# Decoder layer on one core: blocks of the SwiGLU product read ahead of its last writes, weight sums in place, more staging tiles, another order of rooms and of the mixer's first units, a late last norm

## The chip, the core and the metric

The kernel runs on one core of one Trainium2 chip, as one program. The metric is the device time of one execution in microseconds. Three executions of the kernel before gave 2348.09, 2351.1 and 2352.93 us; their median is 2351.1 us. A further execution was profiled, and all rows of the trace come from that one.

## The reference, cut to what matters

The layer has a batch of one, 1024 tokens and 1024 features, all float32:

```python
mod = silu(c) @ w_ada + b_ada                      # nine vectors of 1024: shifts, scales, gates
h = modulate(rmsnorm(x, norm_ffn1), sh1, sc1)
x = x + 0.5 * g1 * swiglu(h, ffn1_w_gate, ffn1_w_up, ffn1_w_down)
h = modulate(rmsnorm(x, norm_mix), sh2, sc2)
x = x + g2 * hybrid_mixer(h, ...)                  # Mamba-2 heads beside latent attention heads
h = modulate(rmsnorm(x, norm_ffn2), sh3, sc3)
x = x + 0.5 * g3 * swiglu(h, ffn2_w_gate, ffn2_w_up, ffn2_w_down)
return rmsnorm(x, norm_final)

def swiglu(h, w_gate, w_up, w_down):               # hidden width 2816
    return (silu(h @ w_gate) * (h @ w_up)) @ w_down
```

## The kernel before, in words

**Arithmetic.** Activations lie transposed: features on the 128 partitions, tokens in the columns, in two halves of 512. Each float32 operand is split in a high part (a cast on ScalarE, L173 for weights) and a low part (a subtraction, L174, on VectorE or, where the caller says so, GpSimd). `mm3` (L182 to L184) makes one product of three passes: high by high, high by low, low by high.

**Seven products for eight.** The two SwiGLU layers group features and tokens in 2x2 blocks and form seven block products. `weight_blocks` (L419 to L440) loads two weight tiles with `raw` (L155 to L160, issued by SP into a ring of four), makes four sums of weight blocks on VectorE (L426) into two tiles `comb`, and splits the blocks on demand: products 1 and 2 together, 6 with 5, 7 with 4, and 3 alone. `seven` (L442 to L489) holds the seven units of twelve matmuls; sums go to a gate result in `g` or an up result in `t`. `gate_up` (L503 to L620) runs over ten pairs of hidden tiles; the last two units of a half are held back behind the first unit of the next. `made` (L529) and `put` (L517) turn the seven sums of each result into high (`gh`, three tiles, L521) and low parts and GpSimd writes both to DRAM (`ab`, L526), 256 KB a write, 14 writes a pair. `pending` holds the puts; two leave after each unit.

**From gate/up to down.** When the last pair is through, the pool of gate/up tiles is closed, `open_down` (L145) opens the weight rooms anew, and `down` (L622) reads the seven blocks of the first of three chunks back, 2 MB each, on GpSimd's queue (`block`, L634 to L639): in the first layer blocks 1, 2, 7 and 4 go to the rooms `bh0`, `bl0`, `bh1`, `bl1` and blocks 6, 5, 3 to `d0`, `d1`, `d2` of the down pool; in the second layer block 1 goes to `d0`, 7 and 4 to `d1` and `d2`, and 2, 6, 5, 3 to `bh1`, `bh0`, `bl0`, `bl1`. The down weights (`r11`, `r21`, `r12`, `r22`, four tiles each, L646) and the residual (L653) come on SP's queue. The units of `down` run in the order of the products 1, 2, 6, 5, 3, 7, 4, four units each; each ends with a gated addition to the residual (L675). The last tokens' half of the second layer is done in two quarters of 256 columns, and each quarter splits its weights anew.

**Rooms.** All rooms are at fixed addresses. The weight pool ends at the top of the memory: before, its gate/up form is 56 KB a partition (`whi`, `wlo`, `comb`, `raw` from low to high) and its down form 44 KB (`r12`, `r22`, `r21`, `wlo`, `whi`, `r11`), so that `r11` lies where `raw` 2 and 3 were. In the second layer the tile that keeps an operand of product 6, `s2`, lies in the gate/up pool at the address that `d0` takes later.

**Side work.** Generators (`side`) are stepped once per unit. `ada_half` (L235, with `ada_add`, L227) loads four tiles of `w_ada` through the same ring `raw`, adds them up on VectorE and ends with small matmuls (L212). `to_mixer` (L1055) writes the new residual out, forms the norm's sums (squares on ScalarE L260, additions on VectorE L264), and makes the normed tiles (L327, L332, L336; for the odd tiles of the first half the low part is GpSimd's, L335, behind an extra ScalarE pass L334). `mixer` (L1118) begins with three weight tiles of 12 matmuls a half-depth for each half of the tokens. `finish` (L1080) scales the first half of the output (L1075), `finish_quarter` the two quarters of the other half.

**Order.** Except in the startup, the order of each engine's instructions is set when the program is built: a planner takes the instructions in the order of the code, with its own estimates of their times, and puts on each engine the first that it thinks is ready. `issue_after` pins a piece of code behind a given instruction of its engine.

## Time and profile before

| what | us |
|---|---|
| median of three executions | 2351.1 |
| the profiled execution | 2346.23 |
| its span, first to last instruction | 2344.5 |
| TensorE (PE) busy in it | 2143.8 |
| VectorE (DVE) busy | 1651.7 |
| ScalarE (ACT) busy | 978.2 |

All times of the trace are counted from the start of the span. The run of stages, by the trace: startup and the first gate/up to 554 us, its down part to 790, the mixer to about 1600, the second gate/up to 2054, its down part and the final norm to 2344.5. Matmuls overlap, so that the time between the starts of two of them, and not the length shown, is what one costs.

### The profile page before, as it was taken

Reading aid. Unit: us, or ns where it says so; the run is one execution under the profiler, and the core shown is the slowest. Engines: PE = TensorE matmul, PEld = TensorE weight load, DVE = VectorE, ACT = ScalarE, POOL = GpSimd, SP = SyncE. Lnnn points to the kernel's source line nnn. Section 1 sums busy time; section 2 is a strip of 40 time slices with the busy share of each in tenths; the row PEclk is TensorE's granted clock in tenths of the full one; section 3 lists DMA queues with packets and bytes.
Section 4 is the critical chain, followed back from the end, with each engine's and each line's share of the span. In section 5 each row is a group of like instructions: output and inputs, shape, how many; then the busy total and the mean of one; then the engine's idle time right before and its main releaser. Section 6 shows DMA issues by size and latency. Waiting matters only on the chain.

```text
span 2344.5 us, 27933 instructions
## 1 busy us (share of the span) xinstructions
PE 2143.8 (91%) x10095; PEld 1745.7 (74%) x10095; DVE 1651.7 (70%) x2797; ACT 978.2 (42%) x1665; POOL 312.7 (13%) x498
## 2 busy tenths in 40 slices
PE   5788999998899799999999999998999999939996
PEld 4666777776688578877778898887777777728875
DVE  7978667675566875456986888869866666545666
ACT  4523444442222442376533767525444444312223
POOL 4111112121000200000212011100111212110000
PEclk9889999999999899999999999999999999969997
DMA  8077645449953343235554000231654545497522
GB/s 292 15 232 231 198 126 171 122 149 345 356 203 120 130 149 107 77 113 173 178 195 123 17 15 22 105 129 60 195 160 130 166 126 171 154 392 260 188 101 72
DMA packets 148345, 367.31 MB, mean 157 GB/s; under 512 B 14080, under 2 KB 39040, under 8 KB 142832
## 3 DMA queue, kind: packets, MB, share of 16 engines
q1 hardware_dynamic: 89200, 182.34, 24.0%
q0 software_dynamic: 54448, 175.60, 22.3%
q10 hardware_dynamic: 4560, 7.60, 0.9%
q8 instruction: 79, 1.29, 0.2%
q14 instruction: 58, 0.48, 0.1%
HBM read 260.69 MB, written 104.79 MB: 156 GB/s over the span
## 4 chain that ended last, share of the span: by engine, by line
PE 40%; issue 35%; DVE 10%; DMA 7%; POOL 6%; ACT 1%; POOLq 0%; SPq 0%; DVEq 0%; ACTq 0%
PE mm L182 7%; PE mm L184 7%; PE mm L183 7%; PE dn L184 5%; PE dn L183 5%; PE dn L182 5%; POOL ab L526 5%; DMA d<-ab 2%; DMA raw<-w_ada 1%; DMA r<-wd 1%; PE dn L1761 1%; DVE acc L891 1%; DVE t L233 1%; DVE wlo L174 1%; DMA M<-ac_d 1%
## 5 line engine op out<-in xcount | busy, mean ns | idle before, releaser
L183 PE MATMUL mm<-bl,whi 128*128 128x512 f32 x1012 | 397.7, 393 | 4.2 <-DVE bl L389 4.2
L182 PE MATMUL mm<-bh,whi 128*128 128x512 f32 x924 | 370.8, 402 | 26.2 <-ACT g L456 11.4
L184 PE MATMUL mm<-bh,wlo 128*128 128x512 f32 x924 | 360.6, 394 | 7.6 <-DVE wlo L174 7.6
L182 PEld LDWEIGHTS mm<-bh,whi 128*128 128x128 f32 x924 | 175.2, 190 | 77.7 <-ACT g L456 15.6
L173 ACT CAST whi<-raw 128x1024 fp32r<-128x1024 f32 (+3 forms) x158 | 136.9, 882 | 225.8 <-PE mm L183 134.8
L183 PEld LDWEIGHTS mm<-bl,whi 128*128 128x128 f32 x1012 | 192.1, 190 | 43.0 <-DVE bl L389 5.1
L182 PE MATMUL dn<-bh,whi 128*128 128x512 f32 x484 | 192.6, 400 | 19.6 <-ACT whi L173 17.3
L184 PEld LDWEIGHTS mm<-bh,wlo 128*128 128x128 f32 x924 | 175.1, 190 | 46.7 <-DVE wlo L174 9.1
L173 ACT CAST whi<-r 128x512 fp32r<-128x512 f32 (+1 forms) x152 | 88.4, 583 | 255.3 <-PE dn L183 119.1
L184 PE MATMUL dn<-bh,wlo 128*128 128x512 f32 x484 | 191.6, 396 | 1.2 <-POOL wlo L174 1.2
L174 DVE TENSOR_TENSOR wlo<-raw,whi 128x1024 fp32r<-128x1024 f32 (+2 forms) x147 | 148.2, 1018 | 47.0 <-ACT whi L173 46.7
L526 POOL DMA_DIRECT2D ab<-gh x154 | 82.0, 533 | 691.3 <-ACT gh L521 677.7
L174 DVE TENSOR_TENSOR wlo<-comb,whi 128x1024 fp32r<-128x1024 f32 x80 | 97.8, 1222 | 104.6 <-ACT whi L173 104.6
L183 PE MATMUL dn<-bl,whi 128*128 128x512 f32 x396 | 157.6, 398 | 4.9 <-DVE bl L330 2.4
L173 ACT CAST whi<-comb 128x1024 fp32r<-128x1024 f32 x80 | 84.2, 1053 | 135.8 <-PE mm L183 125.4
L521 ACT CAST gh<-g 128x512 fp32r<-128x512 f32 x154 | 93.7, 621 | 112.6 <-DVE g L515 77.4
L182 PE MATMUL mm<-x,whi 128*128 128x512 f32 x280 | 115.4, 413 | 12.0 <-ACT g L456 9.8
L182 PEld LDWEIGHTS dn<-bh,whi 128*128 128x128 f32 x484 | 93.3, 193 | 40.8 <-ACT whi L173 18.5
L182 PE MATMUL dn<-d,whi 128*128 128x512 f32 (+1 forms) x200 | 76.5, 383 | 45.5 <-DMA d<-ab 45.0
L184 PE MATMUL mm<-x,wlo 128*128 128x512 f32 x280 | 110.9, 397 | 0.0
L183 PE MATMUL mm<-x,whi 128*128 128x512 f32 x280 | 110.8, 396 | 0.0
L184 PEld LDWEIGHTS dn<-bh,wlo 128*128 128x128 f32 x484 | 92.8, 192 | 21.4 <-POOL wlo L174 1.9
(379 smaller groups left out, 5009.4 us busy)
## 6 DMA issues: line engine op xcount, KB each, us to landing
ab<-gh POOLq DMA_DIRECT2D x154, 256.0 KB, 3.5
ab<-g POOLq DMA_DIRECT2D x154, 256.0 KB, 3.4
raw<-w_ada SPq DMA_DIRECT2D x56, 512.0 KB, 4.2
d<-ab POOLq DMA_DIRECT2D x12, 2048.0 KB, 13.6
raw<-wg SPq DMA_DIRECT2D x44, 512.0 KB, 5.5
raw<-wu SPq DMA_DIRECT2D x44, 512.0 KB, 4.5
r<-wd SPq DMA_DIRECT2D x64, 256.0 KB, 7.8
bl<-ab POOLq DMA_DIRECT2D x8, 2048.0 KB, 10.5
```

The source lines that it names most:

```text
L173: self.made = nc.scalar.copy(out=hi, in_=r)
L174: (engine or nc.vector).tensor_tensor(out=lo, in0=r, in1=hi.bitcast(F32), op=ALU.subtract)
L182: nc.tensor.matmul(out=out, lhsT=ah, rhs=bh, start=first and i == 0, stop=False, skip_group_check=skip)
L183: nc.tensor.matmul(out=out, lhsT=ah, rhs=bl, start=False, stop=False, skip_group_check=skip)
L184: nc.tensor.matmul(out=out, lhsT=al, rhs=bh, start=False, stop=last and i == n - 1, skip_group_check=skip)
L233: engine.scalar_tensor_tensor(out=acc, in0=r, scalar=cj, in1=acc, op0=ALU.mult, op1=ALU.add)
L521: nc.scalar.copy(out=hi, in_=x)
L526: nc.gpsimd.dma_start(out=ab[c][n - 1, :, k, i], in_=y)
L891: nc.vector.scalar_tensor_tensor(out=acc, in0=r, scalar=c, in1=acc, op0=ALU.mult, op1=ALU.add)
L1761: nc.tensor.transpose(out=pt[:, kk * 256 + b * P:kk * 256 + b * P + P], in_=Pt[b][:, (2 * k2 + kk) * P:(2 * k2 + kk + 1) * P], identity=se ...
```

## The change

- Block reads: a pool `lasting` around gate/up and down holds `s2`; it is the room of block 6 in the first layer and of block 1 in the second. Before the last pair's held units the code now reads blocks 1, 2, 6 (first layer), or 1 and 2 and, one unit later, 6 and 5 (second layer). One step of `pending` is left out there.
- Weight sums: made after the split of products 1 and 2, in place in the two raw tiles, with one half-size tile `z` for product 5. Pairs split together are now 1 and 2, 6 and 4, 7 and 3; 5 is alone.
- Rooms: `comb` is 2 KB instead of 4 KB, `gh` has five tiles instead of three, and the down rooms lie in the order `r12`, `r21`, `wlo`, `r22`, `r11`, `whi`. `r11` then lies over `raw` 0, 1 and half of 2, `whi` over the rest of `raw`.
- `ada_half` yields twice more ahead of its matmuls; the burst of steps at the first pair is 15 instead of 11.
- Mixer: the first step of the second half's norm comes behind the splits of the first two weight tiles; the six first units run tile by tile on the lower half of the depth, then on the upper; GpSimd makes no low parts of the norm any more.
- End: the second quarter reuses the split weights of the first (eight casts and eight subtractions less); the scaling of the first half is pinned behind the last subtraction of the first quarter.

The diff, cut to its core:

```diff
-SPREAD = ((1, 3, 5, 7), ())
+SPREAD = ((), ())
@@ open_weights, open_down
-                self.wts.tile([P, size], dt, name=name, bufs=bufs)
+                self.wts.tile([P, 512 if name == "comb" else size], dt, name=name, bufs=bufs)
-        for name, dt, bufs in (("r12", F32, 4), ("r22", F32, 4), ("r21", F32, 4), ("wlo", F32R, 3), ("whi", F32R, 3), ("r11", F32, 4)):
+        for name, dt, bufs in (("r12", F32, 4), ("r21", F32, 4), ("wlo", F32R, 3), ("r22", F32, 4), ("r11", F32, 4), ("whi", F32R, 3)):
@@ ada_half
             yield
+        yield
+        yield
         self.ada_finish(m, half * 4, 4, acc)
@@ weight_blocks
-        ta, tb = [self.wts.tile([P, 1024], F32, name="comb", bufs=2).rearrange("p (a b) -> p a b", b=P) for _ in range(2)]
+        z = self.wts.tile([P, 512], F32, name="comb", bufs=2).rearrange("p (a b) -> p a b", b=P)
-        tt(tb[:, 0:4], b22, b12, ALU.subtract)
-        tt(ta[:, 0:4], tb[:, 0:4], b11, ALU.add)
-        tt(ta[:, 4:8], b12, b11, ALU.subtract)
-        tt(tb[:, 4:8], b21, ta[:, 0:4], ALU.subtract)
-                src, names = next(x for x in ((r1, (1, 2)), (ta, (6, 5)), (tb, (7, 4)), (b22, (3,))) if n in x[1])
+                src, names = next(x for x in ((r1, (1, 2)), (r1, (6, 4)), (z, (5,)), (r2, (7, 3))) if n in x[1])
+                if n == 1:
+                    tt(z, b12, b11, ALU.subtract)
+                    tt(b12, b22, b12, ALU.subtract)
+                    tt(b11, b12, b11, ALU.add)
+                    tt(b21, b21, b11, ALU.subtract)
@@ ffn (block moved here from down), gate_up
+        with self.tc.tile_pool(name=f"lasting{b}", bufs=1, reuse_waits="tile") as bp:
+            def block(c, n, dp=None):
+                if n is None:
+                    return bp.tile([P, KT, 512], F32R, name="s2")
+                name = homes[n]
+                t = (bp if name == "s2" else dp if name[0] == "d" else self.main).tile([P, KT, 512], F32R, name=name)
+                v = t.rearrange("p (k h) n -> p k h n", h=2)
+                self.nc.gpsimd.dma_start(out=v[:, 0:CHUNKS[c]], in_=ab[c][n - 1])
-                hi = tp.tile([P, 512], F32R, name="gh", bufs=3)
+                hi = tp.tile([P, 512], F32R, name="gh", bufs=5)
-                        for _ in range(11):
+                        for _ in range(15):
-        self.weave(held, [side, out])
+        for f in early:
+            f()
+        self.weave(held[:1], [side])
+        for f in early2:
+            f()
+        self.weave(held[1:], [side, out])
@@ down: unit, end
+                elif (n, p) in kept:
+                    hi, lo = kept[n, p]
+                elif w < 512:
+                    np_ = CHUNKS[c]
+                    if p == 0:
+                        kept[n] = self.main.tile([P, KT, 512], F32R, name="bl0") if n == 7 else block(None, None)
+                    t = kept[n].rearrange("p (q i) n -> p q i n", i=2)[:, p, :, 0:np_ * P].rearrange("p i (a b) -> p i a b", b=P)
+                    hi, lo = kept[n, p] = t[:, 0], t[:, 1]
+                    nc.scalar.copy(out=hi, in_=r(src[n]))
+                    self.last_lo = tt(lo, r(src[n]), hi.bitcast(F32), ALU.subtract)
+            self.all_split = self.last_lo.ins
             u = rest(256, 256)
@@ run
-        homes = {1: (0, "bh0"), 2: (0, "bl0"), 6: (1, "d0"), 5: (1, "d1"), 3: (1, "d2"), 7: (0, "bh1"), 4: (0, "bl1")}
+        homes = {1: "bh0", 2: "bl0", 6: "s2", 5: "d1", 3: "d2", 7: "bh1", 4: "bl1"}      # early: ((1, 2, 6), ())
-        next(last)
-        homes = {1: (1, "d0"), 2: (0, "bh1"), 6: (0, "bh0"), 5: (0, "bl0"), 3: (0, "bl1"), 7: (1, "d1"), 4: (1, "d2")}
+        homes = {1: "s2", 2: "bh1", 6: "bh0", 5: "bl0", 3: "bl1", 7: "d1", 4: "d2"}      # early: ((1, 2), (6, 5))
@@ finish, mixer
-        yield from self.write(xT, c0, w, r[0])
+        while self.all_split is None:
+            yield
+        yield from self.write(xT, c0, w, r[0], after=self.all_split)
+            next(norm_h1)
-                self.weave(unit(0) + unit(1) + unit(2), [self.paced(norm_h1, NORM1)] if hh == 0 else [], drain=True)
+                self.weave([u for us in zip(unit(0), unit(1), unit(2)) for u in us], [self.paced(norm_h1, NORM1)] if hh == 0 else [], drain=True)
```

## Rows read from the trace of the kernel before

**Rows 1.** The page: busy us of each engine, its share of the span, instructions.
```profile
PE 2143.8 (91%) x10095; PEld 1745.7 (74%) x10095; DVE 1651.7 (70%) x2797; ACT 978.2 (42%) x1665; POOL 312.7 (13%) x498
```
**Rows 2.** PE's waits, whole run: total us, times, longest us.
```profile
PE dn L182 <- DMA d<-ab: 45.0, 2, 38.0
PE mm L182 <- ACT g L456: 21.2, 20, 2.1
PE dn L182 <- ACT whi L173: 17.7, 3, 14.1
...
PE dn L184 <- DVE wlo L174: 11.6, 7, 6.0
...
PE dn L212 <- DVE t L233: 9.0, 6, 2.9
```
**Rows 3.** Windows: length, busy PE, PEld, DVE, ACT, POOL; PE clock, DMA share, GB/s.
```profile
300.00:500.00 200.00, 194.62 (x841) 155.72 (x840) 132.70 (x185) 85.60 (x126) 36.98 (x70) 1.00 0.48 145
...
554.00:606.00 52.00, 38.07 (x137) 28.98 (x136) 37.43 (x95) 13.46 (x24) 11.16 (x21) 0.87 1.08 408
2054.00:2097.00 43.00, 5.03 (x14) 3.71 (x13) 14.80 (x23) 5.93 (x10) 8.97 (x17) 0.56 1.09 410
790.00:810.00 20.00, 4.74 (x12) 3.06 (x11) 17.72 (x17) 12.60 (x19) 10.31 (x7) 0.57 0.53 201
2309.00:2344.00 35.00, 15.24 (x87) 14.20 (x86) 20.67 (x59) 6.48 (x16) 4.77 (x6) 0.63 0.34 120
```
**Rows 4.** Timeline of PE, 2030 to 2110: start, length, instruction, idle before.
```profile
2039.34 0.39 PE L184 MATMUL mm<-s,wlo 128*128 128x512 f32 x1
...
2092.37 0.77 PE L182 MATMUL dn<-d,whi 128*128 128x512 f32 x1 [37.97 <-DMA d<-ab]
2092.94 0.63 PE L183 MATMUL dn<-d,whi 128*128 128x512 f32 x1
2093.36 0.63 PE L184 MATMUL dn<-d,wlo 128*128 128x512 f32 x1
...
2099.41 0.39 PE L183 MATMUL dn<-d,whi 128*128 128x512 f32 x1
2099.64 0.39 PE L184 MATMUL dn<-d,wlo 128*128 128x512 f32 x1
```
**Rows 5.** Timeline of POOL, 2070 to 2080: the read of block 1.
```profile
2074.04 0.54 POOL L638 DMA_DIRECT2D d<-ab  x1
```
**Rows 6.** Timeline of SP, 2036 to 2075: residual, then down weights.
```profile
2037.04 10.87 SPq L653 DMA_DIRECT2D x<-x_d  x16
2048.29 25.79 SPq L646 DMA_DIRECT2D r<-wd  x16
```
**Rows 7.** DMA issues, 2030 to 2110: count, KB each, median us to landing.
```profile
d<-ab POOLq DMA_DIRECT2D x4, 2048.0 KB, 19.4
```
**Rows 8.** The loads of the down weights (L646), 2036 to 2100.
```profile
DMA to landing us min/median/max: 7.3/9.6/19.6
```
**Rows 9.** Timeline of ACT, 796 to 806: first casts of the mixer's weights.
```profile
803.29 2.92 ACT L173 CAST whi<-raw 128x1024 fp32r<-128x1024 f32 x3
```
**Rows 10.** Groups by line, 785 to 805: busy us, mean ns, idle before.
```profile
L327 DVE SCALAR_TENSOR_TENSOR t<-x,scl,rs 128x512 f32<-128x512 f32 x8 | 7.8, 1004 | 0.1
...
L336 DVE SCALAR_TENSOR_TENSOR bl<-t,mod,bh 128x512 fp32r<-128x512 f32 x4 | 3.0, 740 | 0.0
```
**Rows 11.** Groups by line, 2309 to 2316: the first half's scaling.
```profile
L1075 DVE SCALAR_TENSOR_TENSOR x<-x,kv,rs 128x512 f32<-128x512 f32 x8 | 5.4, 747 | 0.4 <-ACT rs L303 0.4
L174 DVE TENSOR_TENSOR wlo<-r,whi 128x384 fp32r<-128x384 f32 x3 | 1.6, 549 | 0.0
```
**Rows 12.** Groups by line and shape, 400 to 440 (one pair): weights.
```profile
L174 DVE TENSOR_TENSOR wlo<-comb,whi 128x1024 fp32r<-128x1024 f32 x4 | 4.9, 1223 | 6.4 <-ACT whi L173 6.4
...
L173 ACT CAST whi<-comb 128x1024 fp32r<-128x1024 f32 x4 | 4.2, 1054 | 7.8 <-PE mm L183 7.8
...
L426 DVE TENSOR_TENSOR comb<-raw 128x512 f32<-128x512 f32 x4 | 2.7, 687 | 2.4 <-DMA raw<-wg 2.3
```

More of the change, by code (lines that the diff above doesn't have):

```diff
@@ L66 @@
 WPOOL = (12, 13)
-SPREAD = ((1, 3, 5, 7), ())
+SPREAD = ((), ())
 CHUNKS = (4, 4, 3)
+NG = 8
 TWO_PI = 2.0 * math.pi
@@ L529, in made @@
         def made(a, k, p):
-            new = lambda: tp.tile([P, 512], F32, name="g", bufs=8)
+            new = lambda: tp.tile([P, 512], F32, name="g", bufs=NG)
             if k == (0, 1):
@@ L554, in act @@
         def act(ps, t, hh):
-            a = first[t, hh] = tp.tile([P, 512], F32, name="g", bufs=8)
+            a = first[t, hh] = tp.tile([P, 512], F32, name="g", bufs=NG)
             nc.scalar.activation(out=a, in_=ps[0], func=AF.Silu)
@@ L570, in gateup @@
             return [g, u]
-        A = begin(load, gateup_mm, act, gateup, tp)
+        A = begin(load, gateup_mm, act, gateup, bp, tp)
         sums = self.made.ins
         def gate_units(t):
-            us, res = self.seven(A, self.weight_blocks(wg, t), lambda: tp.tile([P, 512], F32, name="g", bufs=8))
+            us, res = self.seven(A, self.weight_blocks(wg, t), lambda: tp.tile([P, 512], F32, name="g", bufs=NG))
             def silu(k):
@@ L620, in gate_up, with down @@
         self.weave([], [side], drain=True)
-    def down(self, ab, xd, wd, b, dp, side, mid, quarters, homes):
+    def down(self, A, block, xd, wd, b, side, mid, quarters):
         nc = self.nc
@@ L632, in down @@
         src = {1: "r11", 2: "r21", 5: "r11", 3: "r22", 7: "r12", 4: "r21"}
-        def block(c, n):
-            pool, name = homes[n]
-            t = (dp if pool else self.main).tile([P, KT, 512], F32R, name=name)
-            v = t.rearrange("p (k h) n -> p k h n", h=2)
-            nc.gpsimd.dma_start(out=v[:, 0:CHUNKS[c]], in_=ab[c][n - 1])
-            A[n] = [(v[:, k, 0], v[:, k, 1]) for k in range(CHUNKS[c])]
         def weights(c, name):
@@ L676, in unit @@
             return go
-        for f in ((block, 1), (weights, "r11"), (block, 2), (weights, "r21"), (block, 6), (weights, "r12"), (weights, "r22")):
-            f[0](0, f[1])
+        for n in (1, 2, 6):
+            if n not in A:
+                block(0, n)
+            for name in {1: ("r11",), 2: ("r21",), 6: ("r12", "r22")}[n]:
+                weights(0, name)
         for n in (1, 6):
             residual(n)
-        block(0, 5)
-        residual(5)
-        block(0, 3)
-        residual(4)
-        block(0, 7)
-        block(0, 4)
+        for n in (5, 3, 7, 4):
+            if n not in A:
+                block(0, n)
+            if n in (5, 4):
+                residual(n)
         then = {5: "r11", 3: "r22", 7: "r12", 4: "r21"}
@@ L1019, in rest, with go @@
             return [(t[:, 4 * i:4 * i + 4, 0:512], t[:, 4 * i:4 * i + 4, 512:1024]) for i in range(2)]
-        def go(load, gateup_mm, act, gateup, tp):
-            s2 = tp.tile([P, KT, 512], F32R, name="s2", bufs=1)
+        def go(load, gateup_mm, act, gateup, bp, tp):
+            s2 = bp.tile([P, KT, 512], F32R, name="s2")
             blocks = self.second_half(xT, r1[0], 0, hT, (s2[:, 0:4], s2[:, 4:8]), rest, tp)
@@ L1040, in rest, with go @@
             return [(x[:, 0:4], x[:, 4:8]) for x in t]
-        def go(load, gateup_mm, act, gateup, tp):
+        def go(load, gateup_mm, act, gateup, bp, tp):
             load(0)
             load(1)
-            s2 = tp.tile([P, KT, 512], F32R, name="s2", bufs=1)
+            s2 = bp.tile([P, KT, 512], F32R, name="s2")
             for hh in range(2):
@@ L1059, in to_mixer, with write @@
         yield from self.ada_norm(xT, 1, hh, self.hT, tp, spread=SPREAD[hh])
-    def write(self, xT, c0, w, r, scaled=(), behind=None):
+    def write(self, xT, c0, w, r, scaled=(), behind=None, after=None):
         nc = self.nc
@@ L1067, in write @@
                 yield
-            after = self.tailed.get(behind)
+            after = self.tailed.get(behind, after)
             with self.tc.issue_after(after) if after is not None and j not in scaled else nullcontext():
```

33 lines of the change are left out of this document (19 added, 14 removed).

## The prediction

> **What bounds the kernel now.** I read the page first: PE is busy for 91% of the span, no other engine for more than 70% [rows 1]. So only time in which PE stands still, or runs at the lower clock, can be won, and I looked next at who PE waits for [rows 2]. Five entries matter: 45.0 us for blocks read back, nearly all in one wait of 38.0; 17.7 for weight casts, 14.1 of it in one wait; 11.6 for low parts, 6.0 in one; 9.0 for the sums of `ada_half`; and 21.2 in twenty waits of about 1 us, one in each pair of the gate/up loops. The windows then show these places against the steady loop [rows 3]. To read them I need the price of a matmul: at the full clock the starts are 0.23 us apart, right after the long wait 0.42 [rows 4]. That is the granted clock's lower level, 1.2 GHz instead of 2.4, after PE had stood still. In the steady loop 841 matmuls x 0.23 are 193 of 200 us: little to win. The handover from gate/up to down of the first layer has 137 x 0.23 = 31.5 us of work in 52, so 20.5 are lost; that of the second 14 x 0.23 = 3.2 in 43, so 39.8 are lost; the mixer's entry 2.8 in 20, so 17.2. In both handovers the DMA engines are full, at 408 and 410 GB/s.
>
> **Second handover.** PE is through at 2092.4 - 38.0 = 2054.4 [rows 4]. Block 1, the first one needed, is issued only at 2074.04 [rows 5] and takes some 19.4 us to land [rows 7]: the start at 2092.4. After the change its room is `s2`, read for the last time by the matmul at 2039.34 [rows 4], so the read can be issued near 2040. It lands between 5.1 us later (2.1 MB at 410 GB/s) and 19.4 later: 2045 to 2059. The weights `r11` are the second condition. Before, SP issued all 16 residual loads first, then the weights from 2048.3 to 2074.1 [rows 6], and they took 7.3 to 19.6 us to land [rows 8]: the first was there by 2067.9 at the latest. With the new rooms most of `r11` lies over raw tiles that are free earlier, and it can go ahead of the residual; a room over the last raw tile would still be late. So PE starts between 2054.4 and 2068. The third condition is product 6, which needs all four kinds of weights: the last of 16 was issued at 2074.1 and landed by 2093.7. If four leave this queue early, the rest come 4 x 25.8 / 16 = 6.4 us sooner, at about 2087, while PE would be ready for product 6 after eight units of 12 matmuls, 22 us after 2054.4, at 2076.5. Before it began 22.1 us after 2092.4, with 39.8 - 38.0 = 1.8 of half clock on top, at 2116.3. Bounds: 24 us (start at 2068 and product 6 at 2092) and 40 (no wait left). I take **31**, near the row of the late weights.
>
> **First handover.** 20.5 us lost: 45.0 - 38.0 = 7.0 for block 6 in `d0`, behind the writes; 17.7 - 14.1 = 3.6 for a cast; the rest is half clock and smaller waits [rows 2, 3]. Block 6 goes to `s2`, and `r11` and `whi` lie over raw tiles, so the cast need not wait. Five `gh` tiles instead of three let the last casts and writes go without waiting for earlier writes to land. Late next is block 5 in `d1`, over the `g` tiles that the last writes read. Ahead of it are 6.3 MB of blocks, 3.7 of writes, 4.2 of weights and 3.1 of residual, 19.4 with itself: 47.5 us at 408 GB/s. The reads can start when PE has done with the rooms of products 1, 2 and 6, five units of 2.76 us before 554, at 540; so block 5 is there near 587.7, and PE wants it at 554 + 33 = 587. There is no margin. Bounds 5 and 20; I take **14**. In both layers `pending` skips one step at the held unit, so two puts come a unit later: nothing waits for them but `d1` and `d2`.
>
> **The mixer's entry.** PE waits 14.1 us for a cast that starts at 803.29 [rows 2, 9], though PE stopped at 790: in code order eight squares of the second half's norm stand ahead on ScalarE. With the step moved behind the splits of two weight tiles, the cast waits only for the load. Then the first half's normed tiles decide. From about 785 VectorE has eight L327, eight L336 (four of them new) and three additions L675, 19 x 0.74 = 14.1 us [rows 10], so it ends near 799; the lower half of the depth is there after eleven of them, near 793, and the new order of units lets PE work on that half for three units. PE began at 803.3 + 1.0 = 804.3, so it can start some 10 us earlier. The third tile's cast stays pinned behind the last square, the second norm must be ready 10 us sooner, and its eight tiles cost VectorE 1.48 us each: I give 2 back. Bounds 2 and 13; I take **8**. While GpSimd made low parts, L327 took 1004 ns on average instead of 740 [rows 10]; this is in the 14.1 us as removed, and if it stays, 8 x 0.26 = 2.1 us are lost and the term is 6. The Trainium skill (SBUF — State Buffer, Who interferes with whom) says that a VectorE instruction with two inputs in SBUF is held while a GpSimd instruction reads SBUF. By that rule the 1004 ns goes with the four GpSimd passes, and the trace agrees as far as this one stretch goes. GpSimd still makes two low parts of weights there.
>
> **The end.** PE waits 6.0 us for a low part [rows 2], because eight scalings of 0.747 us (6.0) are ahead of it on VectorE [rows 11]. The second quarter makes no low parts any more (eight x 0.549 = 4.4 us less on VectorE, as many casts less on ScalarE), so this wait has no object. The scalings still run among that quarter's additions; if these wait, part of the 6.0 comes back. With the half clock after the wait, bounds 2 and 9; I take **6**.
>
> **Sums of `ada_half`.** 9.0 us in six waits [rows 2]. The two yields put the matmuls two units (5.5 us) after the last sums. The longest, 2.9, lies in the burst at the first pair, which runs at one place of the code, so nothing changes there. Bounds 0 and 9; **4**. In the mixer 28 steps meet 24 slots; the rest is drained after the loop, at most one wait of 2.9 there, taken as 0.
>
> **Weight sums, steady loop.** As many sums, casts and subtractions of the same sizes as before; no term. What moves is the order: a first split (1.05 + 1.22) now stands ahead of the four sums (4 x 0.69 = 2.7) [rows 12]. PE has four units of 2.8 us to cover this, and VectorE is busy 133 of 200 us [rows 3]. The raw tiles are held longer, by up to two products. Bounds: 10 gained if earlier casts of `gh` shorten half of the 21.2 us of small waits, 20 lost at 0.5 us for each of 40 blocks. **0**.
>
> **Sum.** 31 + 14 + 8 + 6 + 4 = 63 us. The profiled execution took 2346.2, of which 1.7 lie outside the span; it lies 4.9 below the median of the three. I take the same 63 from the median: 2351.1 - 63 = **2288.1** (2283.2 against the profiled one).
>
> **Rivals.**
> A. *The waits only move.* The reads share the DMA engines with weights, residual and writes, and the weights come no sooner. For it: full engines in both handovers [rows 3], 4.2 MB of weights in 25.8 us, 163 GB/s of 410 [rows 6]. Against it: 24 us of the second handover are won even then. 24 + 5 + 8 + 6 + 4 = 47: 2304. The Trainium skill (DMA: Bandwidth & Descriptors, Queues, rings and completion order) says that each DMA engine takes turns between the queues that have work. By that rule reads on GpSimd's queue slow SP's loads, which is this rival.
> B. *All is hidden.* 40 + 20 + 10 + 8 + 6 = 84: 2267. For it: PE needs 33 us for three products, and 408 GB/s bring 13.5 MB in that time. Against it: the late rooms of `r12` and `r22`.
> C. *The reads do not move.* The planner leaves the reads behind the writes, as for block 1 before [rows 5]; only mixer, end, sums and some 3 us of the cast are won, 21: 2330. Against it: `s2` no longer belongs to the pool whose closing held `d0`.
> D. *Slower.* The in-place sums lose their cover: product 6 of each of 40 blocks waits for all four sums, 2.7 us, 110 in all: 2351.1 - 63 + 110 = 2398. It decides from 63 / 40 = 1.6 us a block. Against it: the cover of four units.
>
> **How the numbers follow.** Forecast 0.45, A 0.25, B 0.20, C 0.05, D 0.05. The likeliest case gives 2288.1. The range 2262 to 2312 holds the forecast, A with 8 us above it for a loss in the steady loop, and B with 5 below it for a gain there; C and D lie outside. The forecast's own range is 2276 to 2300. A measurement of this kernel can tell about 0.2%, 4.7 us, from no change. Only D is slower: 0.05; 0.02 for the same; 0.93 faster.
>
> **What would show it.** PE's wait for `d<-ab` (45.0) should fall under 10, and the read of block 1 stand before the last writes on GpSimd. The 14.1 at the mixer's entry should be under 6, the 6.0 at the end gone, L335 absent, the sums' waits under 6. The gap before product 6 in the second handover tells B from A. Wrong would be: new PE waits in the steady loop (over 1.4 us in a pair more than now), or more than 14 us between the last gate/up matmul and the first down matmul of the second layer.

## The result, and the profile after

The changed kernel takes 2362.4 us (median of four runs) where the kernel before takes 2349.6 beside it: a ratio of 1.0054, interval 1.0036 to 1.0071. It is slower by some 13 us. The prediction was 63 us faster, and none of its rivals gives this number. Both signs that it named as wrong came: PE's waits in the steady loop grew by 1.5 us a pair (from 5.4 to 13.1 us in the five pairs from 300 to 500 us), and 24 us lie between the last gate/up matmul and the first down matmul of the second layer. The profiled execution took 2361.28 us, its span is 2359.5.

To see where the time went I took the start of the same matmul in both traces (10095 in each). The third column is how far the changed kernel is behind; the fourth what the stretch added.

| up to matmul | before, us | after, us | behind | added | stretch |
|---|---|---|---|---|---|
| 900 | 283.8 | 273.7 | -10.1 | -10.1 | startup, first pairs |
| 2000 | 547.3 | 549.2 | +1.9 | +12.0 | steady loop, first layer |
| 2200 | 615.8 | 631.2 | +15.4 | +13.5 | first handover |
| 2900 | 777.0 | 792.2 | +15.2 | -0.2 | first down part |
| 3200 | 864.9 | 876.8 | +11.9 | -3.3 | mixer's entry |
| 7200 | 1605.4 | 1619.5 | +14.1 | +2.2 | mixer |
| 9000 | 2048.4 | 2085.5 | +37.1 | +23.0 | second gate/up |
| 9100 | 2112.4 | 2137.0 | +24.6 | -12.5 | second handover |
| end of span | 2344.5 | 2359.5 | +15.0 | -9.6 | second down part, end |

The page after, as [rows 1]:

```profile
PE 2159.4 (92%) x10095; PEld 1756.3 (74%) x10095; DVE 1649.4 (70%) x2793; ACT 965.2 (41%) x1651; POOL 306.3 (13%) x494
```

The span less PE's busy time is 200.7 us before and 200.1 after: PE stands still as long as it did. The same 10095 matmuls are busy 15.6 us longer, and that is the loss. Most of it is the clock: the mean granted clock is 0.968 before and 0.962 after, and by the trace's clock records the 1.2 GHz level held for 152 us of the span before and 180 after. At half the speed, 27 us more are 14 us of work lost. One stop of 38 us has become two of 24 and 18 us and many short ones, and some of the short ones, too, are followed by a stretch at the lower level. The waits tell where the stops are. PE's waits over the whole run, after the change (total us, times, longest):

```profile
PE dn L184 <- ACT whi L175: 38.3, 5, 23.7
PE mm L184 <- DVE g L457: 30.1, 13, 2.9
PE mm L184 <- DVE x L700: 18.1, 2, 17.9
...
PE dn L186 <- DVE wlo L176: 6.4, 6, 1.7
...
PE dn L214 <- DVE t L235: 4.3, 4, 2.5
```

The 45.0 for `d<-ab`, the 6.0 at the end and half of the sums' 9.0 are gone [rows 2]. In their place stand waits that weren't there: 13 for the addition `g` L457, twelve of them of 2.1 to 2.9 us, one of 17.9 for the additions to the residual, and one of 23.7 for a cast. The windows after, as [rows 3] (columns as there):

```profile
300.00:500.00 200.00, 186.87 (x790) 148.36 (x789) 125.16 (x175) 79.59 (x118) 36.33 (x69) 0.98 0.46 138
556.00:608.00 52.00, 28.68 (x100) 22.23 (x100) 25.74 (x68) 7.57 (x13) 9.59 (x18) 0.74 1.08 402
805.00:825.00 20.00, 8.04 (x20) 5.54 (x19) 18.19 (x21) 11.14 (x17) 6.28 (x3) 0.57 0.59 207
2091.50:2134.50 43.00, 19.09 (x69) 14.79 (x70) 15.86 (x26) 6.62 (x11) 7.43 (x14) 0.68 0.91 329
```

In the steady loop 790 matmuls fit in 200 us instead of 841: 51 x 0.23 = 12 us lost in that stretch alone. The granted clock averages 0.98 there instead of 1.00: PE now stands still for 2 to 3 us once in each pair of this stretch, and after two of the five stops the level is the lower one for 3.4 us. The first handover has 100 matmuls instead of 137. The second has 69 in 43 us instead of 14; 187 would fit at 0.23, so 118 x 0.23 = 27 us are still lost.

**What PE waits for in the steady loop.** VectorE, 396 to 405 us of the changed kernel (start, length, instruction, idle before and releaser):

```profile
396.64 1.42 DVE L430 TENSOR_TENSOR raw<-raw 128x512 f32<-128x512 f32 x2
401.55 0.69 DVE L430 TENSOR_TENSOR comb<-raw 128x512 f32<-128x512 f32 x1 [3.49 <-DMA raw<-wg]
402.16 1.22 DVE L176 TENSOR_TENSOR wlo<-raw,whi 128x1024 fp32r<-128x1024 f32 x1
403.30 0.68 DVE L457 TENSOR_TENSOR g<-g,mm 128x512 f32<-128x512 f32 x1
```

The first sum of the next weight pair, `comb` L430, waits 3.49 us for the load of that pair's second tile. Behind it on VectorE stand a low part and then L457, which empties the PSUM bank PE wants. PE, in the same stretch:

```profile
401.46 0.39 PE L185 MATMUL dn<-bl,whi 128*128 128x512 f32 x1
404.03 0.50 PE L184 MATMUL mm<-bh,whi 128*128 128x512 f32 x1 [2.18 <-DVE g L457]
```

The load is late because its tile is. SP issues it only at 395.53, right behind the last split that reads this tile (its low part ends at 395.5, the first of the two from 394.25), and it lands at 401.5 (VectorE, 394 to 397, then SP, 394 to 404, changed kernel):

```profile
394.25 2.35 DVE L176 TENSOR_TENSOR wlo<-raw,whi 128x1024 fp32r<-128x1024 f32 x2
```

```profile
395.53 0.33 SPq L161 DMA_DIRECT2D raw<-wg  x1
```

VectorE waited for such loads before, too (2.9 us at most, 13.0 in 300 to 500 us), but the addition did not stand behind that wait. Now it waits longer. These are VectorE's waits from 300 to 500 us in the changed kernel:

```profile
DVE comb L430 <- DMA raw<-wg: 18.9, 5, 4.2
```

**What stands at the handovers.** SP's queue at the first handover, before (first fence, 520 to 600 us) and after (second, 536 to 612): start, time over which they are issued, count.

```profile
524.02 31.91 SPq L646 DMA_DIRECT2D r<-wd  x16
556.14 33.55 SPq L653 DMA_DIRECT2D x<-xT  x16
```

```profile
540.29 26.81 SPq L661 DMA_DIRECT2D r<-wd  x16
568.19 40.41 SPq L668 DMA_DIRECT2D x<-xT  x16
```

The weights start 16.3 us later, and so the residual 12.1 us later. What SP waits for in front of the first weight is the last reader of a raw tile (SP's waits, 530 to 612 us, changed kernel):

```profile
SPq L661 <- DVE wlo L176: 35.3, 1, 35.3
```

The additions to the residual then come one per 5.6 us, each held by its load (VectorE, 579 to 598, changed kernel):

```profile
579.63 0.75 DVE L700 SCALAR_TENSOR_TENSOR x<-dn,gat,x 128x512 f32<-128x512 f32 x1 [2.17 <-DMA x<-xT]
585.17 0.75 DVE L700 SCALAR_TENSOR_TENSOR x<-dn,gat,x 128x512 f32<-128x512 f32 x1 [4.80 <-DMA x<-xT]
590.80 0.75 DVE L700 SCALAR_TENSOR_TENSOR x<-dn,gat,x 128x512 f32<-128x512 f32 x1 [4.68 <-DMA x<-xT]
596.35 0.75 DVE L700 SCALAR_TENSOR_TENSOR x<-dn,gat,x 128x512 f32<-128x512 f32 x1 [4.66 <-DMA x<-xT]
```

At the second handover block 1 is issued 14.4 us before PE is through with gate/up at 2091.5, as predicted, and landed at 2088.5. The weights are what is late (GpSimd's and SP's queues):

```profile
2077.12 0.55 POOL L510 DMA_DIRECT2D s<-ab  x1 [16.65 <-issue]
```

```profile
2073.90 19.80 SPq L668 DMA_DIRECT2D x<-x_d  x16
2099.04 22.00 SPq L661 DMA_DIRECT2D r<-wd  x16
```

SP still issues all 16 residual loads first, and these now take 19.8 us to issue instead of 10.87 [rows 6], since from the twelfth on each new one goes out when an earlier one has landed, and in the end these land one per block read. So the first weight goes out at 2099.0, 7.6 us after PE is through; before, it went out 6.1 us ahead of that. Why a load of 256 KB takes as long as a block of 2 MB is in the queues' rows from 580 to 600 us (packets, MB, share of the 16 engines; q0 has the block reads, q1 SP's loads):

```profile
q0 software_dynamic: 504, 7.47, 89.2%
q1 hardware_dynamic: 506, 0.93, 14.1%
```

Both queues move the same number of packets, but a block's packet has 14.8 KB and a load's 1.8 KB.

**The mixer's entry.** ScalarE before the first cast of the mixer's weights, changed kernel:

```profile
810.69 1.14 ACT L264 ACTIVATE t<-x 128x512 f32<-128x512 f32 x2
812.71 0.72 ACT L336 ACTIVATE bh<-t,mod 128x512 fp32r<-128x512 f32 x1 [0.89 <-DVE t L331]
813.34 1.65 ACT L264 ACTIVATE t<-x 128x512 f32<-128x512 f32 x3
814.90 1.03 ACT L175 CAST whi<-raw 128x1024 fp32r<-128x1024 f32 x1
```

Five of the eight squares (L264) still stand ahead of the cast, whose load had landed at 806.9. So do the last four passes L336 of the first half's normed tiles, which wait for VectorE; how much of the delay each of the two makes, no run separates. PE waits 10.5 us instead of 14.1.

### The profile page after: what moved, and what is told of

Same layout as the page of the kernel before. It is cut to its first block, busy times and chain, and to the rows that moved or that the text cites. A ratio compares the mean times of both kernels' runs of the same rounds, so it can differ in the third digit from the quotient of the medians.

```text
span 2359.5 us, 27910 instructions
## 1 busy us (share of the span) xinstructions
PE 2159.4 (92%) x10095; PEld 1756.3 (74%) x10095; DVE 1649.4 (70%) x2793; ACT 965.2 (41%) x1651; POOL 306.3 (13%) x494
## 3 DMA queue, kind: packets, MB, share of 16 engines
q0 software_dynamic: 54448, 175.60, 22.2%
## 4 chain that ended last, share of the span: by engine, by line
PE 61%; DVE 18%; DMA 11%; issue 6%; ACT 2%; SPq 0%; POOL 0%; DVEq 0%; ACTq 0%; POOLq 0%
PE mm L184 12%; PE mm L186 11%; PE mm L185 11%; PE dn L186 7%; PE dn L184 7%; PE dn L185 7%; DVE g L532 5%; DMA raw<-wg 4%; DVE wlo L176 3%; DMA r<-wd 3%; DMA raw<-w_ada 2%; PE dn L1792 1%; DMA x<-xT 1%; DMA x<-x_d 1%; DVE acc L919 1%
## 5 line engine op out<-in xcount | busy, mean ns | idle before, releaser
L185 PE MATMUL mm<-bl,whi 128*128 128x512 f32 x1012 | 403.4, 399 | 4.2 <-DVE bl L393 4.2
L175 ACT CAST whi<-raw 128x1024 fp32r<-128x1024 f32 (+3 forms) x198 | 196.6, 1002 | 329.4 <-PE mm L185 105.0
L176 DVE TENSOR_TENSOR wlo<-raw,whi 128x1024 fp32r<-128x1024 f32 (+3 forms) x187 | 216.3, 1165 | 58.5 <-ACT whi L175 58.3
L184 PE MATMUL dn<-bh,whi 128*128 128x512 f32 x484 | 193.3, 401 | 16.2 <-ACT whi L175 13.7
L175 ACT CAST whi<-r 128x512 fp32r<-128x512 f32 (+1 forms) x136 | 80.3, 591 | 247.6 <-PE dn L185 112.7
L184 PEld LDWEIGHTS dn<-bh,whi 128*128 128x128 f32 x484 | 93.5, 193 | 38.0 <-ACT whi L175 15.5
L700 DVE SCALAR_TENSOR_TENSOR x<-dn,gat,x 128x512 f32<-128x512 f32 (+1 forms) x104 | 73.5, 707 | 55.8 <-PE dn L186 38.9
L176 DVE TENSOR_TENSOR wlo<-r,whi 128x512 fp32r<-128x512 f32 (+1 forms) x136 | 87.1, 643 | 23.4 <-ACT whi L175 23.2
L184 PE MATMUL mm<-bl,whi 128*128 128x512 f32 x212 | 86.0, 406 | 18.7 <-DVE x L700 17.9
## 6 DMA issues: line engine op xcount, KB each, us to landing
bh<-ab POOLq DMA_DIRECT2D x8, 2048.0 KB, 14.5
```

Source lines behind the costliest of these rows:

```text
L175: self.made = nc.scalar.copy(out=hi, in_=r)
L176: (engine or nc.vector).tensor_tensor(out=lo, in0=r, in1=hi.bitcast(F32), op=ALU.subtract)
L184: nc.tensor.matmul(out=out, lhsT=ah, rhs=bh, start=first and i == 0, stop=False, skip_group_check=skip)
L185: nc.tensor.matmul(out=out, lhsT=ah, rhs=bl, start=False, stop=False, skip_group_check=skip)
L700: nc.vector.scalar_tensor_tensor(out=xs, in0=ps, scalar=self.gat[:, 8 * b + o:8 * b + o + 1], in1=xs, op0=ALU.mult, op1=ALU.add)
```

## The experiments

Each ratio is to the kernel before, with its 95% interval, timed beside it on the same chip. The rounds ran on several chips, on which the kernel before took 2349.6 to 2354.8 us (medians), so two medians of different rounds can differ by 5 us for that alone; there the ratios decide. The diffs are cut to their core. "Stage" numbers are from matmul counts as in the table above, from one profiled execution each.

### Sums, staging tiles, reads: one at a time

Theory 1: the in-place sums hold the raw tiles. Theory 2: the reads, rooms and staging tiles cost it. **Sums out of place** in the changed kernel, with three `gh` tiles to make the room (this puts back the old place of the sums, ahead of the first split, and the old pairs of splits as well):

```diff
-        z = self.wts.tile([P, 512], F32, name="comb", bufs=2)
+        ta, tb = [self.wts.tile([P, 1024], F32, name="comb", bufs=2) for _ in range(2)]
...
-                hi = tp.tile([P, 512], F32R, name="gh", bufs=5)
+                hi = tp.tile([P, 512], F32R, name="gh", bufs=3)
```

> The changed kernel with the weight sums out of place again, as before (and three gh tiles, which makes the room for the wider comb). Theory 1, the raw tiles are held too long: in place, a pair's first raw tile is free only after the third product's split, so the second tile of the next pair lands when its sum is already wanted, and at the handovers the rooms over raw tiles come free late. Then a gate/up pair takes 40.0 us again instead of 41.5 to 43.1 (PE's wait for g of the additions gone), the weights of the first down loop are issued near 524 instead of 540, and the time is 2362 - 29 (both steady loops) - 14 (first handover) = about 2319 or less. Theory 2, the early reads and the new rooms cost it, and the fifth gh tile moves the steady loop: the handover stays as it is, and the time is 2345 to 2362.

Measured: 2343.3 us, 0.9947 (0.993 to 0.9963), 25 less than the changed kernel by the ratios. The steady loop is the old one:

```profile
300.00:500.00 200.00, 194.59 (x842) 155.73 (x840) 132.75 (x185) 85.60 (x126) 37.01 (x71) 1.00 0.47 145
```

The loop's part of the theory holds, the handover's does not: two of the `r11` loads go out at 524, but twelve of the sixteen weights only from 553.8, behind a matmul that reads the last split weights, and PE's wait for the residual additions is still 15.8.

**Three `gh` tiles** alone (the control), and **in-place sums alone** on the kernel before:

```diff
-                hi = tp.tile([P, 512], F32R, name="gh", bufs=5)
+                hi = tp.tile([P, 512], F32R, name="gh", bufs=3)
```

> The changed kernel with three gh tiles instead of five, nothing else: the control for the run with the sums out of place. Theory 1: the steady loop keeps its waits of 2 to 3 us a pair, the time is within 6 us of 2362. If the two more staging tiles are what moved VectorE's order in the steady loop, a pair falls back to about 40.0 us and the time to about 2335.

Measured: 2360.7 us, 1.0026 (1.0008 to 1.0044). The waits for `g` L457 stay, but they are shorter (8.1 us instead of 12.4 in 300 to 500 us), and 809 matmuls fit instead of 790:

```profile
300.00:500.00 200.00, 187.92 (x809) 149.66 (x809) 126.51 (x176) 80.97 (x121) 36.46 (x69) 1.00 0.47 141
```

So the staging tiles are not without part in the loop. With three of them the two loops lose 8.9 and 12.7 us to the kernel before, with five 12.0 and 23.0, and the other four runs with in-place sums, four raw tiles and five `gh` tiles give 12.3 to 12.5 and 21.5 to 22.9. These 13 us come back elsewhere: with three tiles the first pairs gain 5 us less, and PE waits 9.7 us in the second layer's next chunk, which with five it does not. Why five lengthen the loop's waits was not separated.

```diff
 the kernel before, with
+        z = self.wts.tile([P, 512], F32, name="comb", bufs=2)
...
+                if n == 1:
+                    tt(z, b12, b11, ALU.subtract)
...
```

> The kernel before with the in-place sums alone (comb of 512 columns; reads, rooms, mixer and end as before). Theory 1: the pairs take 41.5 to 43 us instead of 40.0, some 25 to 30 us over both layers, the loads of the down weights start later, and the time is 2350 + 25 to 45, so 2375 to 2395. Theory 2: no change, 2347 to 2353.

Measured: 2385.9 us, 1.0139 (1.0111 to 1.0167), 31 to 33 us slower. The loops lose 9.3 and 16.8 us. Here the old rooms and the late reads are in place, yet the first handover has the same long wait. Four weights are out by 539, and the other twelve go out only from 564.4 on, where the kernel before issued its last at 555.5:

```profile
PE mm L182 <- DVE x L676: 18.9, 1, 18.9
```

**No early reads** in the changed kernel:

```diff
-    ..., homes, ((1, 2, 6), ()))
+    ..., homes, ((), ()))
-    ..., homes, ((1, 2), (6, 5)))
+    ..., homes, ((), ()))
```

> The changed kernel without the early reads of the blocks in either layer (they are issued where the down part begins, as before; rooms, sums and all else as changed). Theory 1: the first handover stays some 13 us worse than before, because the weights and the residual are late whatever the reads do; the second loses part of its 14 us; 2360 to 2378. Theory 2: the residual loads get ahead of the blocks again, the first handover gives back its 13 us, and the time is about 2349, or a little more where the second handover loses.

Measured: 2382.6 us, 1.0117 (1.0098 to 1.0135), 15 slower than with early reads by the ratios (20 by the medians), at the upper end of theory 1's range or a little above it. Block 1 still goes out at 2076.78, some 14 us before PE is through: it is the room `s2`, not the place in the code, that lets it. PE's wait for the first cast is shorter than with the early reads, 15.4 us instead of 23.7. What came instead is a wait in product 2: VectorE's sums for product 6 wait up to 24.6 us for their weights, and the low part for product 2 stands behind them. PE, 2080 to 2160:

```profile
PE mm L186 <- DVE wlo L176: 27.5, 1, 27.5
PE dn L184 <- ACT whi L175: 15.4, 1, 15.4
```

### SP's queue and the rooms

**Residual behind the weights** in the second layer of the changed kernel:

```diff
-            residual(n)
+            with pinned():   # issue_after(the last weight load), second layer only
+                residual(n)
```

> The changed kernel with the second layer's 16 residual loads pinned on SP's queue behind its first 16 weight loads; nothing else. Theory 3, SP's queue: block 1 was in its room at 2088.5, 3 us before PE was through with gate/up at 2091.5, and PE waited 23.7 us for r11 alone, whose loads stood behind 16 residual loads on SP, of which one landed per block read (5.6 us each) while four blocks of 2 MB came in. Then r11 is issued near 2076 and the wait of 23.7 falls under 8; part of it returns as additions that wait for the residual, as in the first layer (17.9), so the time falls by 5 to 20, to 2342 to 2357. Theory 1 in its strict form (the weights are late because their rooms over the raw tiles come free late): the wait stays over 18 and the time within 5 of 2362.

Measured: 2361.0 us, 1.0032 (1.002 to 1.0045), no gain outside the intervals. The wait of 23.7 fell to 3.3, as theory 3 says, but 10.2 came back as additions that wait for the residual, and 2.9 more by matmul 9500. The profiled execution was the fastest of the six (2356.7), so its trace alone would show a gain of 5 us. Here another order mostly changes which small load is late.

**The old rooms**, with the sums out of place and with the sums in place:

```diff
-  ("r12", F32, 4), ("r21", F32, 4), ("wlo", F32R, 3), ("r22", F32, 4), ("r11", F32, 4), ("whi", F32R, 3)
+  ("r12", F32, 4), ("r22", F32, 4), ("r21", F32, 4), ("wlo", F32R, 3), ("whi", F32R, 3), ("r11", F32, 4)
```

> Sums out of place and three gh tiles (as in the run with the sums out of place, 2343), and in addition the old order of rooms in the down pool (r12, r22, r21, wlo, whi, r11). If the first handover's 12 to 13 us there come from the new rooms (four r11 loads at 524 before, two now, twelve of sixteen weights only from 553.8), the weights are issued at 524 and 537 again, the first residual loads land before the blocks, PE's wait of 15.8 for the additions falls under 4, and the time falls by about 12 to 2331. If the early block reads cause it, the wait stays and the time is within 4 of 2343.

> The changed kernel with the old order of rooms in the down pool, its in-place sums kept: the fourth corner of a square (sums in or out of place, rooms new or old: 2362, 2343 and 2327 are known). If the two costs stand beside each other, this run gives back the same 16 us as with the sums out of place: 2346. If at the first handover either one alone makes the weights late (the kernel before with the in-place sums lost 16 us there in the old rooms), little comes back: 2355 to 2365, and PE's wait for the residual additions stays above 14.

Measured: 2327.5 us, 0.9889 (0.9874 to 0.9903), and 2352.4 us, 1.0003 (0.9988 to 1.0019). So the new rooms cost 14 to 16 us beside out-of-place sums and 10 to 12 beside in-place ones. The second lies between the two outcomes that were written down for it. In the first run PE's wait for the residual additions is 1.2, in the second still 12.6: either cause alone makes weights late, and the costs add only in part. The four corners at the first handover, with the stage's change against the kernel before (matmuls 2000 to 2200):

| sums, rooms, `gh` tiles | PE's wait for residual additions, us | stage, us |
|---|---|---|
| in place, new, five (three) | 17.9 (12.7) | 13.5 lost (11.4 lost) |
| out of place, new, three | 15.8 | 12.5 lost |
| in place, old, five | 12.6 | 3.2 lost |
| out of place, old, three | 1.2 | 5.0 gained |

In the stage the new rooms weigh more than the sums.

**The old rooms, sums out of place and no early reads**; the same with **the residual behind the weights**, the pin (without and with early reads):

> As the run with the sums out of place and the old rooms, and in addition no early block reads: what is left of the change is the mixer's entry, the end, the two yields and s2 as a lasting room. Expected from the first traces: the mixer's entry 3 to 4 us and the end some 8 us gained, nothing at the first handover, at the second block 1 late again (38 us lost as before): 2350 - 12 = 2338, and 14 us worse than with early reads at the second handover. If the early reads are what hurts the first handover, this run is the faster one there by about 12.

> Sums out of place, old rooms, no early reads (2316.6), and the second layer's residual pinned behind its weights. Theory 3: PE's 13.7 us for r11 in the second handover fall under 4; some of it returns as additions that wait for residual: 2303 to 2314. If the reads in flight and not SP's order are the limit: 2314 to 2320.

> Sums out of place, old rooms, early reads, and the second layer's residual pinned behind its weights: the candidate to beat both. Theory 3: both handovers lose their long waits in part, 2331 less 5 to 20, so 2311 to 2326. If the weights' rooms are the limit: 2331.

Measured: 2316.6 (0.9844, 0.9827 to 0.986), 2326.0 (0.9884, 0.9848 to 0.992) and 2320.6 us (0.9855, 0.9837 to 0.9873). Without early reads it is 11 us faster, the other way round from the changed kernel and against what I wrote. Two places of the second layer make this. Counted from the end of gate/up, PE starts the down part 9.6 us later with the early reads: it waits 23.3 us for the cast of `r11` instead of 13.7. Then it waits another 10.8 us from 2132.8 on, because the next chunk's weights come behind the next blocks. VectorE there, with early reads (2125 to 2150):

```profile
DVE t L649 <- DMA r<-wd: 15.7, 2, 15.4
```

In the runs with 2 MB reads and without the pin, the wait for `r11` goes by the early reads of the second layer, whichever the rooms, the sums, the raw and the `gh` tiles. With them it is 23.7, 24.1, 22.2, 23.3, 22.2 and 22.4 us (the changed kernel, sums out of place, three `gh` tiles, old rooms with either sums, five raw tiles). Without them it is 15.4, 13.7, 15.3 and 14.9 us, though block 1 is issued some 14 us before PE is through with gate/up in all ten.

With early reads the pin gives 7 us (2327.5 to 2320.6). Without them it gives nothing, against theory 3 in its simple form (2326.0 against 2316.6 us, from different rounds, with intervals that overlap): in that run 15.6 us came back at 2135.8, in the next chunk.

**Early reads in the first layer only**, without and with the pin:

> Sums out of place, old rooms, early reads in the first layer only. By the progress of the two earlier runs (early in both 2327, in neither 2317): the first layer's early reads left it 3.6 us further ahead at the end of its down part and some 10 at the middle of the second gate/up loop, the second layer's cost 14 in its down part. So about 2307 to 2313. If the first layer's reads give nothing: 2317.

> The same with the second layer's residual pinned behind its weights: both together, 2297 to 2310. If the pin gives nothing without the early reads: as the run beside it.

Measured: 2312.5 (0.9836, 0.9804 to 0.9868) and 2317.3 us (0.9851, 0.9822 to 0.9879). The first is in its range, but the interval doesn't tell it from no early reads at all; the pin again gives nothing, and that run is above its range.

### A fifth raw tile

The in-place sums free 4 KB a partition, which out of place they need themselves. The change gave them to two `gh` tiles; a raw tile is 4 KB too. **Five raw tiles, three `gh` tiles** in the changed kernel, in the best combination, and on the kernel before with the in-place sums alone:

```diff
-        self.open_weights(4, 4, 1024)
+        self.open_weights(5, 4, 1024)
...
-                hi = tp.tile([P, 512], F32R, name="gh", bufs=5)
+                hi = tp.tile([P, 512], F32R, name="gh", bufs=3)
```

> The changed kernel with in-place sums and five raw tiles instead of four (the 4 KB come from three gh tiles instead of five; control: the run with three gh tiles, 2360.7). Theory 1, the held tiles: with a fifth tile the second load of a wg pair need not wait for the split of the third or fifth product, VectorE's sum no longer waits for it (18.9 us in 200 between 300 and 500), a pair takes 40.0 to 40.6 us, and the two loops give back 20 to 29 us: 2332 to 2341. If the loss is the order on VectorE (split first, then the four sums, then PSUM's addition), the pair stays at 41.5 to 43 and the time at 2355 to 2365.

> In-place sums with five raw tiles, old rooms, early reads in the first layer only: the best combination so far (2312 with the sums out of place) with the sums in place again. If a fifth tile takes the whole price of the sums in place: 2308 to 2316. If the order on VectorE costs as well: 2325 to 2340.

> The kernel before with the in-place sums and five raw tiles, three gh tiles as it has, nothing else of the change: without the fifth tile this was 33 us slower than before. If the ring of raw tiles was the whole price, the pairs take 38.8 us as in the run with five tiles (no wait for a sum or a kept copy, 40.0 before), which is 20 to 25 us less in the two gate/up loops, and the reads, rooms, mixer and end stay as before: 2352 - 20 to 30, so 2322 to 2332. If the fifth tile only helps together with the rest of the change: 2345 to 2360.

Measured: 2299.1 us, 0.9775 (0.9757 to 0.9793); 2284.7 us, 0.9719 (0.9697 to 0.9741); 2347.7 us, 0.9972 (0.9956 to 0.9989). The first two beat their ranges. In the first, VectorE's wait of 18.9 us for `raw<-wg` is gone, PE has no wait of note in the loop, and more matmuls fit than before the change:

```profile
300.00:500.00 200.00, 199.31 (x869) 161.22 (x868) 140.35 (x198) 90.05 (x133) 42.24 (x80) 1.00 0.49 149
```

869 - 790 = 79 matmuls x 0.23 = 18 us in 200. The code still puts the first split ahead of the sums, so that order is not what cost the time. The weights of the first handover start at 501.2, and the wait of 17.9 is 3.6. One number differs from the run with three `gh` tiles, the length of the ring, and 61.5 us go with it (59 by the ratios): by the stages 16 and 21 in the two loops, 13 at the first handover and 8 in the first pairs. Theory 1 holds for the loop. On the kernel before with the in-place sums the fifth tile gives 38 us. Against the kernel before itself the loops gain 7.4 and 16.1 us by the same matmul count (900 to 2000, 7400 to 9000), but 14.5 are lost at the first handover (a wait of 16.9 for the additions), and 5 to 8 at the first pairs of each layer, so the total stays above its first range and lies in the second, the one for a fifth tile that helps only together with the rest of the change.

### Reads with shorter rows

Theory 4: the queues take turns by packet. **Each block read as four transfers**, in the changed kernel and in the best version:

```diff
-                self.nc.gpsimd.dma_start(out=v[:, 0:CHUNKS[c]], in_=ab[c][n - 1])
+                for k in range(CHUNKS[c]):
+                    self.nc.gpsimd.dma_start(out=v[:, k:k + 1], in_=ab[c][n - 1][:, k:k + 1])
```

> The changed kernel, each block read as four transfers of 512 KB (4 KB in a row per partition instead of 16); the same bytes. In the changed trace, from 580 to 600, the reads' queue and SP's queue moved 504 and 506 packets but 7.47 and 0.93 MB: turns by packet, 14.8 KB against 1.8. Theory 4, turns by packet: with rows of 4 KB SP gets some 2 of 6 parts, a 256 KB load lands every 1.9 us instead of 5.6, PE's wait for the residual additions in the first handover (17.9) falls under 9 and the wait for r11 in the second (23.7) under 17; both together give 10 to 20 us: 2342 to 2352. If the order of issue alone decides: the waits stay within 3 us and the time within 5 of 2362.

> The best version so far (in-place sums with five raw tiles, old rooms, early reads in the first layer only: 2284.7), each block read as four transfers. Theory 4: the wait for r11 in the second handover (14.9) falls by 4 or more, 2272 to 2281. If the order of issue alone decides, or four times as many issues on GpSimd cost what the turns give: 2282 to 2290.

Measured: 2351.2 us, 0.999 (0.998 to 0.9999), 11 less than the changed kernel by the medians and 15 by the ratios, and 2285.3 us, 0.9706 (0.969 to 0.9723). In the changed kernel the wait of 17.9 fell to 2.2 and that of 23.7 to 11.8; most residual loads of the first handover landed 1.4 to 2.0 us apart. The queues from 580 to 600 us:

```profile
q0 software_dynamic: 1533, 4.47, 61.6%
q1 hardware_dynamic: 1859, 3.37, 49.9%
```

SP's queue moved 3.6 times as much in the same time, with the same bytes to bring in all. In the best version, where no early read runs in the second layer, the wait for `r11` fell from 14.9 to 11.7, less than the 4 us expected, 4.1 came back in product 2, and the time is the same: the second of the two outcomes.

## Why the prediction was wrong, point by point

**Weight sums, steady loop: 0, measured 12.0 and 23.0 lost.** This is the step that decided. It said that the raw tiles are held longer, "by up to two products", and then priced only the work on VectorE, at most 0.5 us a block. What the held tiles delay is the next load: it is issued when a tile is free. The sum waits for that load, and an addition that PE needs stands behind the sum. 35 us over 40 blocks are 0.9 us a block, less than rival D's 1.6, and at another place than D's: it is not product 6 that waits for the sums, but the next result for a PSUM bank. It is shown by the sums out of place (the loop is back at 842 matmuls) and the fifth tile (869). Some 13 of the 35 us come only with five `gh` tiles, which the prediction had as a help.

**First handover: 14 gained, measured 13.5 lost.** The sum counted the bytes up to block 5 at 408 GB/s. It took it that `r11` and `whi` over raw tiles can be written early, and did not ask when SP's loads are issued. The in-place sums hold a raw tile until 540.3, and the new rooms put twelve of the sixteen weights behind the last use of the split weights even without these sums. Then the residual, last on SP, met the block reads. The four corners above show it. The size was too large as well: without both causes the stage gains 5.0 us, not 14.

**Second handover: 31 gained, measured 12.5.** Block 1 came as predicted. The step that failed is that `r11` "can go ahead of the residual": SP kept its order. The room of `r11` did not matter, since the wait is 22.2 us with the old rooms and 23.7 with the new ones. The lower bound of 24 took the weights' times of before [rows 6, 8]. From issue to landing they still took 5.9 to 15.5 us, but the early reads stretched the residual loads ahead of them to as much as 28 us, and with these the issue of the first weight. Without early reads this wait is 13.7 to 15.4.

**Rival A** was nearest in kind: it said that the reads slow SP's loads. It still counted 24 us for the second handover, as if SP's loads kept their old times. The trace gives SP a ninth of the bytes, 0.93 of 8.40 MB. The Trainium skill (DMA: Bandwidth & Descriptors, Queues, rings and completion order) says that an engine drains a whole packet of one queue before it turns to the next. The 504 and 506 packets of 14.8 and 1.8 KB agree with that, and the run with shorter rows does roughly, with 1533 and 1859.

**Mixer's entry: 8, measured 3.3.** The step "the cast waits only for the load" failed: five squares and four passes L336 stayed between. That the pass takes less without GpSimd's low parts held: it was L327 with 1004 ns in [rows 10] and is L331 with 744 now.

**End: 6.** The mechanism is right: the 6.0 wait is gone. The size was a little small: the second down part with the end gained 9.6, above the bound of 9, and all runs with this end gain 9.4 to 11.4 behind matmul 9500.

**Sums of `ada_half`: 4.** The waits fell from 9.0 to 4.3, as predicted. The 10.1 gained up to matmul 900 is more than that, and neither the yields without the in-place sums (0.4 gained) nor the in-place sums alone (0.9 lost) give it. Both together with three `gh` tiles gain 4.8. Runs with the same code up to there differ by as much as 6 us, so the cause stays open.

The bounds could not hold the result: with every term at its lower bound the sum is still 13 us gained, since no term but the steady loop's reached below zero.

## What to carry to other kernels

A sum made in place saves a tile and lengthens the life of another: before pricing it at nothing, read when the loads of that ring are issued, and give the saved room to the ring first (here 4 KB there were worth some 60 us in the changed kernel and 38 in the kernel before with in-place sums, and as staging tiles nothing in the total). In this kernel small loads beside large reads got half the packets and a ninth of the bytes, so look at the packets of each queue in the stretch. Shorter rows in the large transfers helped where large reads ran beside loads that PE waited for, and gave nothing in the best version. Large reads that start earlier can cost more than they bring: in the second layer they added 8 to 10 us to the wait for `r11`. Another order of the small loads gained 7 us in one of four runs and only moved the wait in the others.

## What the hardware showed that was not expected

Two queues with 2 KB and 16 KB rows shared the DMA engines 506 to 504 by packets and 0.93 to 7.47 by MB; with rows of 4 KB it was 3.37 to 4.47. The kernel before has the same cadence of one small load per block in its first handover, only with fewer loads that matter.

At the mixer's entry VectorE's additions of 128x512, 0.69 us in the median, took up to 2.68 us while GpSimd made low parts (VectorE up to 820, then GpSimd, changed kernel):

```profile
814.92 7.04 DVE L268 TENSOR_TENSOR t<-t 128x512 f32<-128x512 f32 x4
```

```profile
816.01 5.41 POOL L176 TENSOR_TENSOR wlo<-raw,whi 128x1024 fp32r<-128x1024 f32 x2 [8.13 <-ACT whi L175]
```

Alone the four would take 2.8 us; two of them took as long as a GpSimd pass each. Whether they would be quick without GpSimd's passes wasn't tried.
